# Branch B's first two weight tiles loaded at the first step of the last gate chunk, and the later ones at the first step of a chunk

## The chip, the core and the metric

The kernel runs on one core of one Trainium2 chip. The metric is the device time of one execution, in microseconds (us). "Before" is the kernel as it stands, "after" the kernel with the change.

## What is computed

One layer of a bidirectional encoder on a 1024 x 1024 float32 input (1024 tokens, model width 1024). A half-step SwiGLU feed-forward block, a normalised projection to queries, keys, values and two gates, two attention branches whose gated outputs are merged, and a second feed-forward block:

```
h = x + 0.5 * SwiGLU_1(RMSNorm(x))
u = RMSNorm(h)
[qA|kA|vA|qB|kB|vB|gA|gB] = u @ W_in
yA = NeighbourhoodAttention2D(qA, kA, vA)          # 8 heads, window in a 16 x 64 grid
yB = WindowedGQA(rope(qB), rope(kB), vB)           # 8 heads, 2 key heads, a sink logit
h = h + (sigmoid(gA) * (yA @ W_A) + sigmoid(gB) * (yB @ W_B)) @ W_out
h = h + 0.5 * SwiGLU_2(RMSNorm(h))
y = RMSNorm_final(h)
```

The part that the change touches is `sigmoid(gB) * (yB @ W_B)`: W_B is 512 x 1024 (`in_w_branch_b`), so `yB @ W_B` is a 512-deep product for 1024 outputs and 1024 tokens.

## The kernel before

**Number format.** Every large product is made of float32 operands split in two: `split` writes a rounded high part on ScalarE (ACT, line 95) and the remainder on VectorE (DVE, line 98). `mm3` (lines 146 to 153) then multiplies high by high, high by low and low by high, so that each 128 x 512 output takes three matmuls on TensorE (PE) for each 128 rows of depth: lines 149, 151 and 153.

**The attention stage.** The loop at lines 1460 to 1486 goes over 32 units of branch B and then 32 of branch A; a unit is 128 queries and one pair of heads. A turn of the loop issues the scores of unit n (`scores`: lines 1401 and 1402 on PE, the biased maximum, line 1406, on DVE, the exponential, line 1409, on ACT), the transposes of the probabilities of unit n-2 (`turn`, line 1422, with the split of the result into two tiles of the pool `ws`) and the product with the values of unit n-3 (`values`, line 1436 or 1441). Between them `filling` draws steps from a second stream, `filler` (lines 1305 to 1327), which keeps PE supplied with dense matmuls.

**The second stream.** `filler` first runs `gate(dc, steps)` for the chunks of the two gates that are still to be made. A chunk is 128 outputs of `u @ W_in`; it has eight steps, each one `mm3` over two banks (six matmuls of 512 columns). `steps` names what else is issued behind a step, mostly loads for later. The last gate chunk loads what branch B needs: the gate of its first chunk (`fetch_gate`), four pieces of yB (`fetch_y`, line 1236, split by `split_y` into `ar` tiles) and weights (`fetch_w`, line 1263). Then `branch_b` runs eight chunks `dc` of 128 outputs of `yB @ W_B`, four steps each. Chunk `dc` reads the weight tile `mix["w", dc]`, and at its end line 1294 multiplies its two banks by the opened gate. Two chunks of branch A are begun in the same way.

**Weight tiles.** Their split parts were made early in the kernel and parked in device memory (`wab_d`). `fetch_w(i)` takes one of the eight buffers of the pool `ws` and loads 128 x 1024 floats (512 KB) from `wab_d[i]`. The same eight buffers hold the two weight tiles of a gate chunk and the tiles that `turn` writes.

**Queues.** Loads and stores that are written `nc.sync.dma_start` are issued by SyncE (SP) one after the other: when one has to wait for its buffer or for the data it reads, all behind it wait too. Stores of finished gate chunks (line 1223) and the loads of branch A's heads (lines 1185 and 1188) are issued by GpSimd (POOL) in the same manner. The order on each engine's queue is set when the kernel is built, by a scheduler that takes the program's order and the buffers' release into account.

Names used below: "the first tile", "the second tile" and so on are the weight tiles of branch B's chunks dc = 0, 1, ...; in the trace all of them are `ws<-wab_d`.

Of the kernel before, what the change touches and what calls it, by code (L numbers as in the profile page):

```python
# [15 lines left out]
P = 128  # L16
# [15 lines left out]
def f32v(ap):  # L32
    return ap.bitcast(F32)
# [3 lines left out]
def trunk_kernel(ctx, tc, x, xt, n1, wg1, wu1, wd1, nm, win, rpb, sink, wa, wb, wo,  # L37
# [35 lines left out]
    def new_ar(g, dt=F32R):  # L73
        ar[g] = main.tile([P, 4, 1024], dt, tag=f"ar{g}", bufs=1, name=nm_("ar"))
        return ar[g]
# [4 lines left out]
    def bank(tag):  # L80
        return ps.tile([P, 512], F32, tag=tag, name=nm_(tag))

    def raw4():
        return main.tile([P, 1024], F32, tag="raw", bufs=4, name=nm_("raw"))

    def xs4():
        return main.tile([P, 1024], F32, tag="xs", bufs=2, name=nm_("xs"))

    def ws4():
        return main.tile([P, 1024], F32R, tag="ws", bufs=8, name=nm_("ws"))  # L90
# [55 lines left out]
    def mm3(banks, first, last, lhs, rhs, **kw):  # L146

        for b, r in zip(banks, rhs):
            nc.tensor.matmul(b, lhs[0], r[0], start=first, stop=False, **kw)  # L149
        for b, r in zip(banks, rhs):  # L150
            nc.tensor.matmul(b, lhs[0], r[1], start=False, stop=False, **kw)  # L151
        for b, r in zip(banks, rhs):
            nc.tensor.matmul(b, lhs[1], r[0], start=False, stop=last, **kw)  # L153

    def drain(gen, n=1 << 30):

        for _ in range(n):
            if next(gen, gen) is gen:
                return
# [949 lines left out]
    def gate_load(k):  # L1109
        hl = [ws4() for _ in range(2)]  # L1110
        for a, src in zip(hl, (wg_d[k, 0], wg_d[k, 1])):
            nc.sync.dma_start(f32v(a), src)
        mix["gate"] = [a.rearrange("p (c f) -> p c f", f=P) for a in hl]
# [93 lines left out]
    def u_half(c, n):  # L1207
        h, l = rhs(((B11, T4), (B21, B22))[c // 4][n])
        return h[:, c % 4, :], l[:, c % 4, :]

    def gate(dc, steps):

        w = mix.pop("gate")
        bs = [bank("g"), bank("g")]
        for k, c in enumerate((4, 5, 6, 7, 0, 1, 2, 3)):
            mm3(bs, k == 0, k == NC8 - 1, (w[0][:, c, :], w[1][:, c, :]), [u_half(c, n) for n in range(2)])
            yield
            if k in steps:
                steps[k]()
        gt = xs4()  # L1220
        for n in range(2):
            nc.scalar.copy(gt[:, n * 512:(n + 1) * 512], bs[n])
        nc.gpsimd.dma_start(g_d[dc * P:(dc + 1) * P, :], gt)
# [3 lines left out]
    def branch_mm(bs, w, y):  # L1227

        for c in range(4):
            mm3(bs, c == 0, c == 3, (w[0][:, c, :], w[1][:, c, :]),  # L1230
                [[slot(k)[:, n * 512:(n + 1) * 512] for k in y[c]] for n in range(2)])
            yield

    def fetch_y(r0):
        mix["y", r0] = raw4()
        nc.sync.dma_start(mix["y", r0], y_d[r0:r0 + P, :])

    def split_y(slots, r0, eng):

        h, l = [slot(k) for k in slots]  # L1240
        r = mix.pop(("y", r0))
        if r0 < 512:
            r = in_block(r)
            h, l = by_block(h), by_block(l)
        split(h, l, r, eng, True)
# [3 lines left out]
    def branch_a(i):  # L1249

        bs = [bank("dg"[i % 2]) for _ in range(2)]
        a_mm.append((bs, branch_mm(bs, mix.pop(("w", NC8 + i)), Y_A)))

    def merged(dc):
        return slot((0, 1, 2, 3, 24, 25, 26, 27)[dc])

    def fetch_gate(dc):
        r = mix["rb", dc] = xs4() if dc % 3 else masks[:, :1024]
        nc.sync.dma_start(r, g_d[D + dc * P:D + (dc + 1) * P, :])

    def fetch_w(i):
        t = ws4()
        nc.sync.dma_start(f32v(t), wab_d[i])
        mix["w", i] = [t[:, k:k + 512].rearrange("p (c f) -> p c f", f=P) for k in (0, 512)]

    def open_gate(dc):
        r = mix["rb", dc]
        pin(nc.scalar.activation(r, r, AF.Tanh, scale=0.5))

    def branch_b():  # L1270

        for g in (0, 6):
            new_ar(g, F32)
        fetch_w(1)
        for dc in range(NC8):
            bs = [bank("g") for _ in range(2)]
            mm = branch_mm(bs, mix.pop(("w", dc)), Y_B)
            for c in range(4):
                drain(mm, 1)
                yield  # L1280
                if c == (0 if dc else 2) and dc + 2 < NC8:
                    fetch_gate(dc + 2)
                if c == 0 and dc == 0:
                    split_y(Y_B[3], 3 * P, nc.vector)
                if c == 1:
                    if dc == 0:
                        open_gate(0)
                    fetch_w(dc + 2)
                elif c == 3 and dc + 1 < NC8:
                    open_gate(dc + 1)  # L1290
            rb = mix.pop(("rb", dc))
            for n in range(2):
                sl = slice(n * 512, (n + 1) * 512)
                nc.vector.scalar_tensor_tensor(out=merged(dc)[:, sl], in0=rb[:, sl], scalar=1.0, in1=bs[n],
                                               op0=ALU.add, op1=ALU.mult)

    def a_fetch(i):
        mix["ra", i] = raw4()
        nc.sync.dma_start(mix["ra", i], g_d[a_order[i] * P:(a_order[i] + 1) * P, :])

    def a_open(i):
        r = mix["ra", i]
        pin(nc.scalar.activation(r, r, AF.Tanh, scale=0.5))

    def filler():
        for dc, nxt in zip(gates, gates[1:] + [None]):
            if nxt is not None:
                yield from gate(dc, {2: lambda: gate_load(gates.index(nxt))})
            else:
                yield from gate(dc, {0: lambda: fetch_gate(0),  # L1310
                                     1: lambda: [fetch_y(c * P) for c in range(2)],
                                     2: lambda: [fetch_y(2 * P), fetch_w(0)],
                                     3: lambda: split_y(Y_B[0], 0, nc.vector),
                                     4: lambda: [split_y(Y_B[1], P, nc.vector), fetch_y(3 * P)],
                                     5: lambda: fetch_gate(1),
                                     6: lambda: split_y(Y_B[2], 2 * P, nc.vector)})
        yield from branch_b()
        for i in range(2):
            branch_a(i)
            for c in range(3):  # L1320
                drain(a_mm[i][1], 1)
                yield
                if c == 0:
                    fetch_w(NC8 + 2 + i)
                    a_fetch(i)
        for i in range(2):
            a_open(i)

    fill = filler()


# [345 lines left out]
```

## Time and profile before

| what | value |
|---|---|
| median of 3 runs | 1925.99 us (1922.42 to 1926.06) |
| the profiled execution | 1925.74 us |
| its span, from the first to the last instruction | 1924.0 us |
| mean granted TensorE clock | 0.997 |
| PE busy | 1910.7 us, 99% of the span |
| DVE, ACT, POOL busy | 1455.9, 947.1, 306.3 us |

The page of the profile gives busy time by engine, the chain of work that ended last, the costliest groups of instructions with the idle time ahead of them, and DMA traffic. The trace also answers which instruction waited for which, what stood on an engine in a given stretch of time, and how busy each engine was there, with the granted clock. Times in such rows are microseconds from the span's start. PE, PEld, DVE, ACT, POOL and SP are the engines; SPq is SP's queue. 1.74 us of the profiled execution lie outside its span.

### The profile page before, as it was taken

What the parts mean: (1) busy time and instruction counts of PE and PEld (TensorE: products, weight loads), DVE (VectorE), ACT (ScalarE), POOL (GpSimd) and SP (SyncE); (2) the same over time, 40 slices, a digit from 0 to 9 for tenths busy, and PEclk for the clock granted to TensorE, in tenths of its full rate; (3) what the DMA queues carried; (4) which work ended last, traced back from release to release, by engine and by line L of the source; (5) the groups of instructions that cost most, each with busy time, mean ns of one, the idle gap of its engine ahead of it and who ended that gap; (6) DMA issues with size and microseconds to landing.
All of it is one profiled execution on the core that took longest, in us unless ns stands there. A gap on an engine that the chain in (4) does not pass through costs nothing.

```text
span 1924.0 us, 25681 instructions
## 1 busy us (share of the span) xinstructions
PE 1910.7 (99%) x8908; PEld 1595.2 (83%) x8908; DVE 1455.9 (76%) x2551; ACT 947.1 (49%) x1852; POOL 306.3 (16%) x476
## 2 busy tenths in 40 slices
PE   9999999999999999999999999999999999999998
PEld 7888888888888888888898888888888888888886
DVE  8988766668967878645888897999675566569864
ACT  7533444444446543434888784475333333344453
POOL 0012222214400112211112101010110001005210
PEclk9999999999999999999999999999999999999999
DMA  6256656687454367734448968543432323492341
GB/s 268 94 174 220 232 193 224 199 294 263 125 171 142 114 203 240 237 110 151 150 117 227 254 190 313 178 156 121 148 107 102 121 88 109 148 357 93 117 141 60
DMA packets 165538, 334.36 MB, mean 174 GB/s; under 512 B 17056, under 2 KB 70688, under 8 KB 165408
## 3 DMA queue, kind: packets, MB, share of 16 engines
q1 hardware_dynamic: 132736, 233.08, 37.2%
q0 software_dynamic: 31952, 98.59, 15.4%
q8 instruction: 70, 1.15, 0.3%
q10 hardware_dynamic: 720, 1.05, 0.1%
q14 instruction: 60, 0.49, 0.1%
HBM read 228.33 MB, written 106.10 MB: 174 GB/s over the span
## 4 chain that ended last, share of the span: by engine, by line
PE 96%; DVE 2%; DMA 1%; issue 0%; ACT 0%; SPq 0%; POOLq 0%; POOL 0%; DVEq 0%
PE g L149 18%; PE g L151 17%; PE g L153 17%; PE d L149 12%; PE d L153 12%; PE d L151 12%; PE d L1422 2%; PE g L1441 1%; PE d L1401 1%; PE g L1436 1%; PE d L1402 1%; DMA ws<-wab_d 1%; PE d L142 1%; DVE ar L98 0%; DMA fx<-in_xt_dram 0%
## 5 line engine op out<-in xcount | busy, mean ns | idle before, releaser
L149 PE MATMUL g<-ar,ws 128*128 128x512 f32 x1096 | 419.4, 394 | 3.4 <-DMA ws<-wab_d 3.4
L151 PE MATMUL g<-ar,ws 128*128 128x512 f32 x1096 | 415.6, 391 | 0.1
L153 PE MATMUL g<-ar,ws 128*128 128x512 f32 x1096 | 414.2, 391 | 0.0
L149 PE MATMUL d<-ar,ws 128*128 128x512 f32 x752 | 291.3, 391 | 0.4 <-ACT ar L889 0.2
L151 PE MATMUL d<-ar,ws 128*128 128x512 f32 x752 | 290.4, 389 | 0.3 <-DVE ar L891 0.3
L153 PE MATMUL d<-ar,ws 128*128 128x512 f32 x752 | 290.3, 389 | 0.2 <-DVE ws L322 0.2
L151 PEld LDWEIGHTS g<-ar,ws 128*128 128x128 f32 x1096 | 206.0, 188 | 41.9 <-DVE ar L98 0.3
L153 PEld LDWEIGHTS g<-ar,ws 128*128 128x128 f32 x1096 | 205.7, 188 | 42.2
L149 PEld LDWEIGHTS g<-ar,ws 128*128 128x128 f32 x1096 | 203.1, 188 | 40.8 <-issue 3.7
L322 DVE TENSOR_TENSOR ws<-raw,ws 128x512 fp32r<-128x512 f32 x222 | 151.8, 689 | 94.7 <-ACT ws L319 93.8
L319 ACT CAST ws<-raw 128x512 fp32r<-128x512 f32 x222 | 136.3, 620 | 152.1 <-PE g L153 70.0
L149 PEld LDWEIGHTS d<-ar,ws 128*128 128x128 f32 x752 | 141.0, 188 | 30.5 <-ACT ar L889 0.6
L151 PEld LDWEIGHTS d<-ar,ws 128*128 128x128 f32 x752 | 141.2, 188 | 30.1 <-DVE ar L891 0.9
L153 PEld LDWEIGHTS d<-ar,ws 128*128 128x128 f32 x752 | 141.2, 188 | 29.8 <-DVE ws L322 0.7
L95 ACT CAST ws<-raw 128x512 fp32r<-128x512 f32 x98 | 61.0, 622 | 119.8 <-PE d L153 61.4
L98 DVE TENSOR_TENSOR ws<-raw,ws 128x512 fp32r<-128x512 f32 x98 | 74.0, 755 | 43.5 <-ACT ws L95 43.4
L426 POOL DMA_DIRECT2D hid<-fx x91 | 49.1, 540 | 349.9 <-DVE fx L486 237.7
L98 DVE TENSOR_TENSOR ws<-ar,ws 128x512 fp32r<-128x512 f32 x114 | 93.6, 828 | 14.5 <-ACT ws L95 14.5
L95 ACT CAST ar<-raw 128x512 fp32r<-128x512 f32 (+1 forms) x81 | 54.1, 670 | 84.3 <-PE g L151 51.4
L149 PE MATMUL g<-ws,ws 128*128 128x512 f32 x232 | 90.9, 392 | 0.0
L153 PE MATMUL g<-ws,ws 128*128 128x512 f32 x232 | 90.4, 390 | 0.0
L151 PE MATMUL g<-ws,ws 128*128 128x512 f32 x232 | 90.3, 389 | 0.0
(325 smaller groups left out, 3678.5 us busy)
## 6 DMA issues: line engine op xcount, KB each, us to landing
raw<-hid SPq DMA_DIRECT2D x70, 512.0 KB
hid<-fx POOLq DMA_DIRECT2D x91, 256.0 KB, 2.9
ar<-in_ffn_w_down_dram SPq DMA_DIRECT2D x32, 512.0 KB
raw<-in_ffn_w_up_dram SPq DMA_DIRECT2D x31, 512.0 KB
raw<-in_ffn_w_gate_dram SPq DMA_DIRECT2D x27, 512.0 KB
hid<-fa POOLq DMA_DIRECT2D x51, 256.0 KB, 2.7
ar<-zs_d POOLq DMA_DIRECT2D x48, 256.0 KB, 6.7
raw<-in_w_in_dram SPq DMA_DIRECT2D x20, 512.0 KB
```

Of the source, the lines that this page charges most:

```text
L95: hi = nc.scalar.copy(dst_hi, src)
L98: (eng or nc.vector).tensor_tensor(dst_lo, src, f32v(dst_hi), op=ALU.subtract)
L142: nc.tensor.transpose(pt[:, c * P:(c + 1) * P], xs[:, (half * 4 + c) * P:(half * 4 + c + 1) * P], ident)
L149: nc.tensor.matmul(b, lhs[0], r[0], start=first, stop=False, **kw)
L151: nc.tensor.matmul(b, lhs[0], r[1], start=False, stop=False, **kw)
L153: nc.tensor.matmul(b, lhs[1], r[0], start=False, stop=last, **kw)
L319: nc.scalar.copy(w[0][:, :512], a)
L322: nc.vector.tensor_tensor(w[0][:, 512:], a, f32v(w[0][:, :512]), op=ALU.subtract)
L426: nc.gpsimd.dma_start(hid[PRODUCTS.index(p), i], src)
L1401: nc.tensor.matmul(b[:, :nw], un["q"][s], un["kd"][s][:, k0 * P:k1 * P], start=True, stop=False)
L1402: nc.tensor.matmul(b[:, :nw], un["q"][s], un["kl"][s][:, k0 * P:k1 * P], start=False, stop=True)
L1422: nc.tensor.transpose(pt[:, i * P:(i + 1) * P], un["pr"][s][:, i * P:(i + 1) * P], ident)
```

## The change

In the last gate chunk the loads of branch B's first and second weight tile are both issued behind the first step (step 0), with the load of the gate. Before, the first tile was loaded behind the third step and the second at the start of `branch_b`, after the eighth step. In `branch_b` the load of tile dc + 2 moves from the second step of chunk dc to the first.

```diff
@@ branch_b
         for g in (0, 6):
             new_ar(g, F32)
-        fetch_w(1)
         for dc in range(NC8):
...
                 if c == 0 and dc == 0:
                     split_y(Y_B[3], 3 * P, nc.vector)
-                if c == 1:
-                    if dc == 0:
-                        open_gate(0)
+                if c == 1 and dc == 0:
+                    open_gate(0)
+                if c == 0:
                     fetch_w(dc + 2)
                 elif c == 3 and dc + 1 < NC8:
                     open_gate(dc + 1)
@@ filler
             else:
-                yield from gate(dc, {0: lambda: fetch_gate(0),
+                yield from gate(dc, {0: lambda: [fetch_gate(0), fetch_w(0), fetch_w(1)],
                                      1: lambda: [fetch_y(c * P) for c in range(2)],
-                                     2: lambda: [fetch_y(2 * P), fetch_w(0)],
+                                     2: lambda: fetch_y(2 * P),
                                      3: lambda: split_y(Y_B[0], 0, nc.vector),
```

The only queue whose order changes is SP's; PE, DVE, ACT and POOL issue the same instructions in the same order as before. Lines behind 1274 have a number lower by one after the change (1372 is 1371, and so on). This is SP's queue in the last gate chunk and up to the third tile, before; `ws_9175` is the first tile, `ws_9380` the second, `ws_9472` the third, and `xs_9522` the gate of the third chunk:

```order
L1236 DMA raw_9123<-y_d 128x1024
L1236 DMA raw_9125<-y_d 128x1024
L1236 DMA raw_9173<-y_d 128x1024
L1259 DMA xs_9302<-g_d 128x1024
L1263 DMA ws_9175<-wab_d 128x1024
...
L1191 DMA raw_9964<-z_d 128x1024
L1263 DMA ws_9380<-wab_d 128x1024
L1259 DMA xs_9522<-g_d 128x1024
L1263 DMA ws_9472<-wab_d 128x1024
L1372 DMA y_d<-fa 64x2x512
```

The same places on SP's queue after the change, where `ws_9091` is the first tile, `ws_9093` the second and `ws_9438` the third:

```order
L1236 DMA raw_9127<-y_d 128x1024
L1236 DMA raw_9129<-y_d 128x1024
L1263 DMA ws_9091<-wab_d 128x1024
L1263 DMA ws_9093<-wab_d 128x1024
L1236 DMA raw_9177<-y_d 128x1024
L1259 DMA xs_9304<-g_d 128x1024
...
L1191 DMA raw_9966<-z_d 128x1024
L1259 DMA xs_9522<-g_d 128x1024
L1263 DMA ws_9438<-wab_d 128x1024
L1371 DMA y_d<-fa 64x2x512
```

The first tile goes ahead of two loads, the second ahead of ten; the third tile stays where it was, behind the gate's load `xs_9522`. Further down the queue, from chunk 4 on, the load of a weight tile and that of a gate change places, at chunk 6 also a weight tile and a store; the rows from there, before:

```order
L1236 DMA raw_10312<-y_d 128x1024
L1259 DMA masks_5583<-g_d 128x1024
L1263 DMA ws_10139<-wab_d 128x1024
L1372 DMA y_d<-fa 64x2x512
L1259 DMA xs_10244<-g_d 128x1024
L1263 DMA ws_10292<-wab_d 128x1024
```

The same rows after the change:

```order
L1236 DMA raw_10312<-y_d 128x1024
L1263 DMA ws_10072<-wab_d 128x1024
L1259 DMA masks_5583<-g_d 128x1024
L1371 DMA y_d<-fa 64x2x512
L1263 DMA ws_10246<-wab_d 128x1024
L1259 DMA xs_10244<-g_d 128x1024
```

Here the weight tile moves one place ahead of a gate's load. On PE the order is unchanged; these are the first matmuls of branch B's second chunk, behind the scores of an attention unit, before:

```order
L1402 MATMUL d_9512<-ar_5099,ar_564 128x384
L149 MATMUL g_9547<-ar_4722,ws_9380 128x512
L151 MATMUL g_9547<-ar_4722,ws_9380 128x512
L153 MATMUL g_9547<-ar_4722,ws_9380 128x512
L1422 MATMUL d_9532<-ident,fa 128x128 x3
```

The same rows after the change:

```order
L1401 MATMUL d_9512<-ar_5099,ar_564 128x384
L149 MATMUL g_9547<-ar_4722,ws_9093 128x512
L151 MATMUL g_9547<-ar_4722,ws_9093 128x512
L153 MATMUL g_9547<-ar_4722,ws_9093 128x512
L1421 MATMUL d_9532<-ident,fa 128x128 x3
```

They read the second tile, which is `ws_9380` before and `ws_9093` after; nothing else differs.

## The prediction

> **What bounds the kernel now.** I read the page first, for the engine that sets the end:
>
> ```profile
> span 1924.0 us, 25681 instructions
> PE 1910.7 (99%) x8908; PEld 1595.2 (83%) x8908; DVE 1455.9 (76%) x2551; ACT 947.1 (49%) x1852; POOL 306.3 (16%) x476
> PE 96%; DVE 2%; DMA 1%; issue 0%; ACT 0%; SPq 0%; POOLq 0%; POOL 0%; DVEq 0%
> L149 PE MATMUL g<-ar,ws 128*128 128x512 f32 x1096 | 419.4, 394 | 3.4 <-DMA ws<-wab_d 3.4
> ```
>
> PE is busy for 99% of the span and is 96% of the chain that ended last. A change elsewhere counts only where it takes away a time in which PE stands still. The last row names one: of all the idle time ahead of line 149's gate matmuls, 3.4 us were ended by the landing of a weight tile `ws<-wab_d`, which is what the change moves. Next I asked PE's waits, to see whether that is one wait or many:
>
> ```profile
> PE g L149 <- DMA ws<-wab_d: 3.4, 1, 3.4
> PE g L810 <- POOL ident masks.py:199: 1.5, 1, 1.5
> PE d L151 <- DVE ar L891: 0.3, 1, 0.3
> ```
>
> The columns are total, count and longest. It is one wait of 3.4 us, the longest in the kernel. PE's timeline shows where it is, with start, duration and, in brackets, the idle time and what ended it:
>
> ```profile
> 1071.19 0.33 PE L1401 MATMUL d<-ar,ar 128*128 128x384 f32 x1
> 1071.36 0.34 PE L1402 MATMUL d<-ar,ar 128*128 128x384 f32 x1
> 1075.13 0.77 PE L149 MATMUL g<-ar,ws 128*128 128x512 f32 x1 [3.43 <-DMA ws<-wab_d]
> 1075.69 0.63 PE L151 MATMUL g<-ar,ws 128*128 128x512 f32 x1
> 1076.12 0.63 PE L153 MATMUL g<-ar,ws 128*128 128x512 f32 x1
> ...
> 1081.01 0.39 PE L151 MATMUL g<-ar,ws 128*128 128x512 f32 x1
> 1081.24 0.39 PE L153 MATMUL g<-ar,ws 128*128 128x512 f32 x1
> ...
> 1089.93 0.40 PE L149 MATMUL g<-ar,ws 128*128 128x512 f32 x1
> ```
>
> The matmul at 1075.13 is the first of branch B's second chunk; the one at 1089.93 is the first of the third chunk, which starts without a wait. Two things are lost at 1071. PE stands still, and then it runs slowly: from L151 to L153 takes 0.43 us at 1075.69 and 0.23 us at 1081.01. The stage table has the granted clock beside it (columns: stretch, length, busy time of PE, PEld, DVE, ACT and POOL, clock, DMA share, GB/s):
>
> ```profile
> 1066.00:1071.50 5.50, 5.44 (x31) 4.46 (x29) 5.11 (x13) 5.43 (x14) 0.00 (x0) 1.00 1.09 361
> 1071.36:1075.13 3.77, 0.34 (x3) 0.05 (x2) 2.92 (x10) 1.84 (x4) 0.00 (x0) 0.87 1.38 239
> 1075.13:1081.01 5.88, 5.88 (x17) 4.84 (x18) 2.52 (x6) 3.59 (x8) 0.00 (x0) 0.50 0.95 262
> 1081.01:1089.93 8.92, 8.92 (x61) 8.09 (x59) 6.02 (x19) 6.31 (x18) 0.14 (x1) 1.00 0.63 210
> 1071.36:1089.93 18.57, 15.14 (x79) 12.98 (x78) 11.45 (x34) 11.73 (x29) 0.14 (x1) 0.82 0.88 232
> ```
>
> The clock is 0.50 for 5.88 us behind the wait and 1.00 before and after. Last, the chain in order of time, and then SP's timeline, say which load it was:
>
> ```profile
> 1058.45 16.55 DMA ws<-wab_d
> 1074.99 0.14 issue
> ```
>
> ```profile
> 1040.20 1.28 SPq L1236 DMA_DIRECT2D raw<-y_d  x3
> 1041.65 0.91 SPq L1259 DMA_DIRECT2D xs<-g_d  x1
> 1042.68 0.53 SPq L1263 DMA_DIRECT2D ws<-wab_d  x1
> ...
> 1058.45 0.37 SPq L1263 DMA_DIRECT2D ws<-wab_d  x1
> 1070.55 0.32 SPq L1259 DMA_DIRECT2D xs<-g_d  x1
> 1070.97 0.37 SPq L1263 DMA_DIRECT2D ws<-wab_d  x1
> 1071.44 0.70 SPq L1372 DMA_DIRECT2D y_d<-fa  x1
> 1082.10 0.32 SPq L1236 DMA_DIRECT2D raw<-y_d  x1
> ```
>
> The awaited load was issued at 1058.45 and took 16.55 us. On SP it is the second `ws<-wab_d` of branch B: the second tile, the one that the change puts at the head of the queue. The third tile went out at 1070.97.
>
> **The second tile, early.** After the change SP issues the first and second tile behind two loads of `y_d`, so at about 1041 and 1041.5, 17 us earlier than the second goes out now. PE needs it at 1071.4, some 30 us later, and even another 16.55 us would be over by 1058.1. The wait then goes. What it gives back: with the clock up, the next matmul would start 0.17 us behind L1402 at 1071.36 (the step from L1401 to L1402), so at 1071.53 and not at 1075.13: 3.60 us. The 5.88 us at half clock hold work that takes 5.88 x 0.23 / 0.43 = 3.15 us at full clock: 2.73 us. Together 6.33 us.
>
> Of the half-clock stretch the Trainium skill (TensorE: Matmul & The Clock Gate, section on Part 1, the HAM clock gate) says that the clock comes back after some 3.4 us of sustained matmuls. By that the second part would be an estimated 1.7 us and the gain 5.3. The trace shows 5.88 us at 0.50, so the sum keeps 2.73.
>
> **What takes the wait's place on PE.** ACT and DVE must keep up through the same instructions. Over 1071.36 to 1089.93 PE would need 18.57 - 6.33 = 12.24 us; ACT is busy for 11.73 and DVE for 11.45. That is 96% and 94%, tight, but before the wait ACT was busy for 5.43 of 5.50 us (99%) and PE did not wait. ACT's and DVE's long idle times in this stretch come from PE's own:
>
> ```profile
> 1077.42 0.48 ACT L95 CAST ws<-d 128x384 fp32r<-128x384 f32 x1 [3.94 <-PE d L1422]
> 1077.94 0.56 DVE L98 TENSOR_TENSOR ws<-d,ws 128x384 fp32r<-128x384 f32 x1 [3.66 <-ACT ws L95]
> ```
>
> ACT waited 3.94 us for PE's transposes, and DVE 3.66 us for ACT. With PE running on, both vanish. The cost lies between 0 and what they would keep of their idle time; I take 0.3 us, near the lower end, by the row at 99% without a wait. That leaves 6.33 - 0.3 = 6.0 us.
>
> **What is moved back.** On SP two issues go ahead of the third `y_d` load, the gate's load and the bias loads: about 0.43 us each (three issues in 1.28), nothing of it on PE. Their data, 1.05 MB, go ahead too. A full stretch moves
>
> ```profile
> DMA packets 596, 2.09 MB, mean 418 GB/s; under 512 B 64, under 2 KB 103, under 8 KB 595
> ```
>
> in 5 us (1045 to 1050), so the third `y_d` piece lands 2.5 us later and the rest 1.25 us later (the first tile was among them anyhow). The pieces of `y_d` are read from
>
> ```profile
> 1065.38 1.04 ACT L95 CAST ar<-raw 128x1024 fp32r<-128x1024 f32 x1
> ```
>
> 24 us behind the issue at 1041, so 0. Were that cover gone, the price would be at most those 2.5 us. SP could also stand at the first tile until a buffer of `ws` is free:
>
> ```profile
> SPq L1263 <- PE g L1436: 13.5, 6, 5.1
> SPq L1259 <- DMA g_d<-xs: 11.7, 1, 11.7
> SPq L1236 <- DMA y_d<-fa: 18.1, 3, 9.8
> ```
>
> The longest wait of that kind now is 5.1 us (first row); behind it stand the same loads, with the same cover, so between 0 and 5.1 us on SP and 0 on PE.
>
> **The third tile and later ones.** Its program place is earlier, but on SP it still stands behind the gate's load of 1070.55, which waited 11.7 us for POOL's store of the last gate chunk (second row). So it goes out at about 1071 as now. Behind it in the queue is the store of 1071.44, and the load of 1082.10 waited for that store's landing (third row; 9.8 us from the issue before it). So the third tile was in by about 1082.1, even with the second one's 512 KB ahead of it, which are now gone from there. PE needs it at 1089.93 - 6.33 = 1083.6: cover of at least 1.5 us. All other weight tiles go out at the same place or earlier, and PE waits for none of them now: 0.
>
> Sum: 1925.74 - 6.0 = **1919.7 us**, made against the profiled execution, which is 0.25 us under the median of the runs (1925.99). The measurement of this kernel can tell about 0.2% (3.9 us) from no change.
>
> **Rivals.** *ACT and DVE hold PE back.* For it speaks the 96%; against it the rows without waits at 99%. If ACT keeps half of its idle time in this stretch (18.57 - 11.73 = 6.84, half is 3.4), the stretch takes 11.73 + 3.4 = 15.1 us instead of 12.24, and the gain is 3.4: 1922.3.
>
> *The third tile takes the second one's place, and it is slower.* SP reaches it only when POOL's store has landed, and it needs no more than the second tile's 16.55 us to miss: 1070.97 + 16.55 = 1087.5, a wait of 3.9 us and again 2.7 at half clock, 6.6 against 6.33 saved: 1926.0, no change. If the tiles that now load early hold up POOL's store by 3 us more, it lands at 1090.5, the wait is 6.9 and the sum 9.6: 1929.0. It decides against the change from a landing later than 1083.6 + 3.6 = 1087.2. Against it: the bound of 1082.1, and 512 KB less in the queue.
>
> **Chances.** The forecast 0.77, the first rival 0.10, the third tile as late as 1087 0.05, later than that 0.08. The forecast and a little of the first rival make faster by over 0.2%: 0.78. The rest of the first rival (1922.3 is 0.19% under the median) and the tile at 1087 make no difference: 0.14. Slower: 0.08. For the range, the low end is the whole 6.33 and half of the spread of the three runs (3.64 / 2 = 1.8): 1917.6, rounded to 1917.5. The high end takes in the first rival, 1922.3, with 0.7 for that spread: 1923.0. Outside are the second rival, 0.13, and some 0.06 at the ends.
>
> **What would show it.** Right: no row `PE g L149 <- DMA ws<-wab_d` among PE's waits, a clock of 1.00 from 1060 to 1090, the first matmul of the third chunk near 1083.6 to 1084, a span near 1918. In SP's timeline the two first tiles go out within 2 us of 1041. Wrong in size: PE waits of some tenths on DVE or ACT behind 1071, with the third chunk's start later than 1085. Wrong altogether: a row of 3 us or more for `ws<-wab_d` at the third chunk, with the clock at 0.50 behind it, or a wait on `ar` near 1066.

## The result and the profile after

The changed kernel takes 1920.01 us (median of 13 runs) against 1924.99 us for the kernel before (13 runs beside it). The ratio is 0.9974, with a 95% interval of 0.9966 to 0.9983: 5.0 us less, between 3.3 and 6.5. One execution of 2259.9 us, at a granted clock of 0.794, is left out of the ratio; the others of the changed kernel lie between 1918.82 and 1922.11, those of the kernel before between 1922.42 and 1928.51. The profiled execution took 1920.27 us.

The page and PE's waits of the changed kernel, the rows that answer to those of before:

```profile
span 1918.5 us, 25682 instructions
PE 1909.1 (100%) x8908; PEld 1593.7 (83%) x8908; DVE 1455.8 (76%) x2551; ACT 947.1 (49%) x1852; POOL 305.6 (16%) x476
L149 PE MATMUL g<-ar,ws 128*128 128x512 f32 x1096 | 418.3, 393 | 0.0
PE g L810 <- POOL ident masks.py:199: 1.5, 1, 1.5
PE d L151 <- DVE ar L891: 0.3, 1, 0.3
```

The span is 5.5 us shorter. PE's busy time is 1.6 us less for the same 8908 matmuls, and the stretch at half clock behind the wait is gone. The idle time ahead of line 149 is 0.0 where it was 3.4, and the row for `ws<-wab_d` among PE's waits is gone; the longest wait that is left, 1.5 us at the kernel's start, was there before.

PE's timeline at the start of the second chunk, and at that of the third (start, duration):

```profile
1072.25 0.34 PE L1401 MATMUL d<-ar,ar 128*128 128x384 f32 x1
1072.42 0.40 PE L149 MATMUL g<-ar,ws 128*128 128x512 f32 x1
...
1084.44 0.40 PE L149 MATMUL g<-ar,ws 128*128 128x512 f32 x1
```

The first product of the second chunk starts 0.17 us behind the score matmul. From there to the third chunk it takes 1084.44 - 1072.42 = 12.02 us; before it was 1089.93 - 1075.13 = 14.80. The stage table over the same place (length, busy time of PE, PEld, DVE, ACT and POOL, clock, DMA share, GB/s):

```profile
1066.00:1071.36 5.36, 5.28 (x31) 4.53 (x31) 4.98 (x13) 5.31 (x12) 0.27 (x1) 1.00 1.24 341
1071.36:1083.60 12.24, 12.24 (x77) 10.89 (x76) 11.87 (x37) 11.46 (x29) 0.00 (x0) 1.00 0.93 205
```

PE is busy for all of the 12.24 us and the clock is 1.00. DVE is at 97% and ACT at 94%, and PE waits for neither. SP's timeline shows where the loads went:

```profile
1041.06 0.81 SPq L1236 DMA_DIRECT2D raw<-y_d  x2
1041.96 1.46 SPq L1263 DMA_DIRECT2D ws<-wab_d  x2
1043.47 0.55 SPq L1236 DMA_DIRECT2D raw<-y_d  x1
...
1072.10 0.32 SPq L1259 DMA_DIRECT2D xs<-g_d  x1
1072.52 0.37 SPq L1263 DMA_DIRECT2D ws<-wab_d  x1
```

The first two tiles go out at 1041.96 and 1042.45 (the row above merges them), the third one at 1072.52.

### The profile page after: what moved, and what is told of

It is laid out like the page before. It is cut to its first block, busy times and chain, and to the rows that moved or that the text cites. A ratio compares the mean times of both kernels' runs of the same rounds, so it can differ in the third digit from the quotient of the medians.

```text
span 1918.5 us, 25682 instructions
## 1 busy us (share of the span) xinstructions
PE 1909.1 (100%) x8908; PEld 1593.7 (83%) x8908; DVE 1455.8 (76%) x2551; ACT 947.1 (49%) x1852; POOL 305.6 (16%) x476
## 3 DMA queue, kind: packets, MB, share of 16 engines
q8 instruction: 70, 1.15, 0.2%
## 4 chain that ended last, share of the span: by engine, by line
PE 97%; DVE 2%; DMA 0%; issue 0%; ACT 0%; SPq 0%; POOLq 0%; POOL 0%; DVEq 0%
PE g L151 18%; PE g L149 18%; PE g L153 18%; PE d L149 12%; PE d L153 12%; PE d L151 12%; PE d L1421 2%; PE d L1400 1%; PE g L1440 1%; PE g L1435 1%; PE d L1401 1%; PE d L142 1%; DVE ar L98 0%; DMA fx<-in_xt_dram 0%; PE d L1199 0%
```

## Experiments: is it the second tile alone?

**The kernel before, once more.** No edit.

> The kernel before, once more, for a second look at the stall. If the stall belongs to the program, PE again waits for the second weight tile of branch B, between 2.5 and 4 us, and runs behind it at a clock of 0.50 for 5 to 7 us. If the 3.4 us of the first profile were a chance of that execution, the wait is under 2 us here and the clock stays at 1.00.

Measured: 1928.57 us, one execution. PE's wait in it, and the load that ended it from the chain (issue, duration):

```profile
1078.11 0.76 PE L149 MATMUL g<-ar,ws 128*128 128x512 f32 x1 [5.56 <-DMA ws<-wab_d]
1059.28 18.69 DMA ws<-wab_d
```

The stall belongs to the program, but its size does not. The load took 18.69 us here against 16.55 in the first profile, and the wait was 5.56 us against 3.43.

**The second tile early, nothing else.**

```
-        fetch_w(1)
...
-                yield from gate(dc, {0: lambda: fetch_gate(0),
+                yield from gate(dc, {0: lambda: [fetch_gate(0), fetch_w(1)],
```

> Half of the change alone: the second weight tile of branch B at the first step of the last gate chunk; the first one stays at its third step, and the later ones at the second step of a chunk, as before. My theory (all of the gain is the second tile's landing): no wait for ws<-wab_d on PE at 1071, the clock 1.00 there, and 5 to 6.4 us less than before, the same as the whole change. The rival (the first tile's place or the later tiles bring part of it): a gain of 3 us or less, or a wait for the first or the third tile.

Measured: 1919.96 us against 1925.71 for before on the same chip, ratio 0.9967 (0.9955 to 0.9980). In its profile PE waits for no tile, and the only wait over 0.3 us is the 1.5 us at the kernel's start that all of them have. This part of the change is worth all of it.

**The later tiles early, nothing else.**

```
-                if c == 1:
-                    if dc == 0:
-                        open_gate(0)
+                if c == 1 and dc == 0:
+                    open_gate(0)
+                if c == 0:
                     fetch_w(dc + 2)
```

> The other half alone: branch B's later weight tiles at the first step of a chunk; the first and second tile as before. My theory: 0. PE waits 3.4 us for the second tile as before and then runs at 0.50 for some 6 us; the time is that of before within 1 us. The rival (the later tiles carry a part of the gain): 2 us or more below before.

Measured: 1926.42 us against 1925.71, ratio 1.0003 (0.9994 to 1.0011). PE's wait is still there:

```profile
1076.21 0.47 PE L149 MATMUL g<-ar,ws 128*128 128x512 f32 x1 [3.85 <-DMA ws<-wab_d]
```

The later tiles' part is worth nothing that can be measured. The third part, the first tile's new place, was not run alone; with that tile in its old place the second tile's load gave the whole gain, so nothing is left for it to explain.

## Experiments: how early is early enough?

**Four places earlier on SP, and one.** In the kernel before, the second tile's load leaves the head of branch B and goes to the sixth step of the last gate chunk (ahead of a bias load, a store and two loads of `z_d`), or to the seventh (ahead of the last load of `z_d` alone):

```
-        fetch_w(1)
...
-                                     5: lambda: fetch_gate(1),
+                                     5: lambda: [fetch_gate(1), fetch_w(1)],
```

```
-        fetch_w(1)
...
-                                     6: lambda: split_y(Y_B[2], 2 * P, nc.vector)})
+                                     6: lambda: [split_y(Y_B[2], 2 * P, nc.vector), fetch_w(1)]})
```

> The kernel before with the second tile only one to four loads earlier on SP: at the sixth step of the last gate chunk, ahead of a bias load, the store of y_d and two loads of z_d that it stood behind. In the profile of before those landed from 1061 to 1071; the tile would take their place and land near 1066 to 1069. My theory (a tile that lands before 1071 is as good as one that lands at 1050): no wait of PE for it, clock 1.00, 1920 us like the whole change. The rival (it must be out of this queue altogether): a wait of 1 us or more remains, 1921.5 or above.

> The kernel before with the second tile exactly one load earlier on SP: the seventh step of the last gate chunk, it changes places with the load of z_d of 1058.01, which landed 3.9 us ahead of it in the first profile (1071.1 and 1075.0). It should land 1 to 2.5 us sooner and leave a wait of 1 to 2.5 us. My theory (the clock drops only where PE stood still for most of one period of 3.4 us): clock 1.00 throughout, only the wait remains, 1921 to 1922.5. The rival of my prediction (half clock of 2.7 us behind any wait): 1923.7 to 1925.2. If PE doesn't wait at all the time is that of the whole change, 1920, and this says nothing on the clock.

Measured: 1920.96 us, ratio 0.9970 (0.9960 to 0.9981), for the sixth step and 1920.90 us, ratio 0.9975 (0.9965 to 0.9986), for the seventh, against 1925.99. Neither profile has a wait for a tile. PE's waits, SP's timeline and one of SP's waits of the second one:

```profile
PE g L810 <- POOL ident masks.py:199: 1.5, 1, 1.5
PE d L151 <- DVE ar L891: 0.5, 2, 0.3
...
1055.83 0.55 SPq L1263 DMA_DIRECT2D ws<-wab_d  x1
1057.95 0.32 SPq L1191 DMA_DIRECT2D raw<-z_d  x1
1069.96 0.32 SPq L1259 DMA_DIRECT2D xs<-g_d  x1
...
SPq L1191 <- DVE s L1365: 1.8, 1, 1.8
```

A change of places with one load of the same size is enough. I had expected a wait of 1 to 2.5 us to be left, by the 3.9 us between the two landings; the load also went out at 1055.83 instead of 1058.45, since SP's wait at that load of `z_d` (1.8 us here, the last row) now stands behind the tile and not ahead of it. How much each of the two brings was not separated. Being this near may have a price: one of the eight runs took 1923.6 us, where nine of the whole change end at 1922.2 (the last experiment). That run has no trace, so a late tile in it is not shown. The test of the clock that this run was also meant for gave nothing, since PE did not wait.

## Experiments: what a late tile costs

**Work in the place of the wait.** 14 products more ahead of the second chunk's first one, and then 7, in the kernel before. Products and other work around them also change places on PE, DVE and ACT, so only the clock, the wait and the sum are read here.

```
             mm = branch_mm(bs, mix.pop(("w", dc)), Y_B)
+            for _ in range(14 if dc == 1 else 0):
+                nc.tensor.matmul(bs[0], slot(4)[:, :P], slot(4)[:, :512], start=True, stop=True)
```

> The kernel before with 14 products more, 128x128 by 128x512, ahead of the second chunk's first one; they write a bank that the chunk's own first product overwrites. They are some 3.2 us of PE's work where PE would wait 3.4 us, and they don't bring the tile earlier. My theory (the stall costs twice: 3.6 us of standing still and 2.7 us of half clock): the tile lands at 1075 as before, but the clock stays at 1.00 behind it, and the time is 2 to 3 us below before in spite of the work added. The rival (the half clock is no consequence of the stand-still, or PE's clock comes down with any late load): clock 0.50 behind the landing as before, and a time equal to before or up to 3.2 us above. If the added products are spread so that PE still stands for over 2.5 us, the test says nothing.

Measured: 1922.46 us against 1925.71, ratio 0.9983 (0.9974 to 0.9992): more work, and a shorter time. The stage table, with the wait:

```profile
1077.43 0.73 PE L149 MATMUL g<-ar,ws 128*128 128x512 f32 x2 [0.61 <-DMA ws<-wab_d]
...
1073.80:1077.21 3.41, 3.02 (x16) 2.20 (x14) 3.11 (x11) 3.39 (x8) 0.00 (x0) 1.00 1.37 240
1077.21:1080.62 3.41, 3.19 (x19) 2.89 (x20) 1.75 (x4) 1.43 (x3) 0.00 (x0) 1.00 1.05 261
```

The tile is as late as ever (PE starts on it at 1077.43), but the clock stays at 1.00. So the half clock is a consequence of PE's standing still, and it is a cost of its own. (The profiled execution, 1924.31 us, is the slowest of the eleven.)

> The kernel before with 7 products more ahead of the second chunk's first one, half of the 14 of the other run; the chunk's own first product overwrites what they write. They are some 1.6 us of PE's work, so of the waits of 3.4 to 5.6 us seen so far 1.8 to 4 us should be left. My theory (the clock drops at the end of one of its periods of 3.41 us in which PE worked for about a third or less, and for nothing shorter): with a wait up to 1.6 us the clock stays at 1.00; with one of 1.8 to 2.2 us it drops only if nearly all of it lies in one period; with more it drops as before, for one or two whole periods, 3.4 or 6.8 us. The time between that of 14 products (1922.5) and before (1925.7). The rival (any wait over 0.6 us is followed by half clock for about as long again): 0.50 behind each of them, its length going with the wait.

Measured: 1923.69 us against 1926.40, ratio 0.9989 (0.9980 to 0.9998), between the two as expected. In the profiled execution (1925.79 us) a wait of 2.84 us was left:

```profile
1077.38 0.51 PE L149 MATMUL g<-ar,ws 128*128 128x512 f32 x1 [2.84 <-DMA ws<-wab_d]
...
1074.80:1078.21 3.41, 0.83 (x4) 0.69 (x5) 2.76 (x8) 2.80 (x7) 0.00 (x0) 1.00 1.25 233
1078.21:1081.62 3.41, 3.41 (x13) 3.03 (x12) 1.13 (x4) 0.02 (x1) 0.00 (x0) 0.50 0.88 307
1081.62:1085.03 3.41, 3.41 (x24) 3.14 (x23) 1.66 (x5) 2.64 (x8) 0.00 (x0) 1.00 0.36 116
```

The stretches are cut where the clock changes. It came down at 1078.21, 0.8 us after PE had gone back to work, and it went up again 3.41 us later. That is not a clock that falls when PE stops and rises when it starts.

**The second tile later still.** Its load behind the gate's load at 1070.6:

```
-        fetch_w(1)
...
                     split_y(Y_B[3], 3 * P, nc.vector)
+                    fetch_w(1)
```

> The kernel before with the second tile made later still: its load stands behind the gate's load at 1070.6 on SP, directly ahead of the third tile's. It would land near 1081, a wait of PE of 8.5 to 10 us instead of 3.4. My theory (the half clock has a size of its own: it ends at the end of the first period of 3.4 us in which PE was busy throughout, 3.4 to 6.8 us behind the restart, and so costs 1.6 to 3.2 us however long the wait was): a clock of 0.50 from about 2.5 us into the wait until 3.4 to 6.8 us behind its end, and a time 5 to 7 us above before, about 1931. The rival (the half clock grows with the wait, 2.7 us for each 3.6): 10 us or more above, 1936.

Measured: 1929.42 us against 1924.99, ratio 1.0023 (1.0014 to 1.0032). The wait, the load, and the stretches:

```profile
1078.91 0.76 PE L149 MATMUL g<-ar,ws 128*128 128x512 f32 x1 [6.27 <-DMA ws<-wab_d]
1071.60 7.17 DMA ws<-wab_d
...
1072.74:1076.16 3.42, 0.00 (x0) 0.00 (x0) 2.48 (x10) 1.56 (x2) 0.00 (x0) 1.00 1.18 238
1076.16:1079.57 3.41, 0.66 (x2) 0.59 (x3) 0.00 (x0) 0.00 (x0) 0.00 (x0) 0.50 1.01 402
1079.57:1082.99 3.42, 3.42 (x13) 2.74 (x12) 0.76 (x2) 1.78 (x5) 0.00 (x0) 0.50 0.44 140
1082.99:1086.40 3.41, 3.41 (x22) 2.99 (x21) 2.98 (x9) 2.78 (x6) 0.00 (x0) 1.00 0.10 38
```

The time is 4.4 us above before, under the 5 to 7 of the theory and far from the 10 of the rival. I had the wait too long: 6.27 us, not 8.5 to 10, since the load took 7.17 us from its issue at 1071.60 where the one issued at 1058.45 took 16.55. The clock came back as the theory said, 4.1 us behind the restart, at the end of the first period in which PE was busy throughout. The wait is 2.8 us longer than in the first profile, and PE's work at half clock is shorter: 0.66 + 3.42 = 4.08 us.

**The clock goes by periods of 3.41 us.** The same cuts in the first profile of before, in its second one, and in that of the later tiles alone:

```profile
1070.74:1074.15 3.41, 0.96 (x5) 0.55 (x3) 3.35 (x12) 2.46 (x5) 0.00 (x0) 1.00 1.40 257
1074.15:1077.57 3.42, 2.44 (x7) 1.94 (x8) 0.13 (x2) 0.15 (x1) 0.00 (x0) 0.50 1.19 219
1077.57:1080.98 3.41, 3.41 (x11) 2.93 (x10) 2.49 (x6) 3.41 (x8) 0.00 (x0) 0.50 0.81 294
```

```profile
1069.92:1073.33 3.41, 2.63 (x14) 1.99 (x12) 3.35 (x9) 3.05 (x10) 0.00 (x0) 1.00 1.20 299
1073.33:1076.75 3.42, 0.00 (x0) 0.00 (x0) 1.80 (x7) 1.01 (x2) 0.00 (x0) 1.00 1.42 234
1076.75:1080.14 3.39, 2.03 (x7) 1.67 (x7) 0.00 (x0) 0.00 (x0) 0.00 (x0) 0.50 1.10 255
1080.14:1083.54 3.40, 3.40 (x12) 2.83 (x11) 2.07 (x5) 3.14 (x8) 0.00 (x0) 0.50 0.58 212
```

```profile
1070.54:1073.95 3.41, 1.83 (x9) 1.25 (x7) 3.35 (x11) 3.07 (x7) 0.00 (x0) 1.00 1.32 269
1073.95:1077.36 3.41, 1.15 (x7) 0.99 (x8) 0.98 (x5) 0.19 (x1) 0.00 (x0) 1.00 1.29 233
1077.36:1080.76 3.40, 3.40 (x13) 2.84 (x12) 2.19 (x6) 3.25 (x8) 0.00 (x0) 0.50 0.99 325
```

Read each row as a period: what PE did in it decides the clock of the next. Behind periods in which PE was busy for 0, 0.83, 0.96 and 1.15 of 3.41 us the clock is 0.50; behind those with 1.83 and 2.63 us it stayed at 1.00. Once at 0.50, it stays there behind periods with 0.66, 2.03 and 2.44 us of work and goes back behind those that were busy throughout.

The trace also keeps the times at which the granted clock changed, and they show that the periods form one grid through the whole execution. In the first profile of before the clock rose at 5.78 us, fell at 1074.15, rose at 1080.98 and fell behind PE's last work at 1920.66: 313, 315 and 561 periods of 3.4133 us after the first rise. In all thirteen traces every later change lies within 0.01 us of a whole number of periods behind the first. The end of the kernel, where PE runs out of work, narrows the limit. These are the last periods there of the run with the tile one place earlier, and of the run with the third tile late (below):

```profile
1909.92:1913.33 3.41, 1.38 (x7) 0.80 (x5) 1.44 (x2) 1.45 (x3) 0.76 (x3) 1.00 0.41 154
1913.33:1916.74 3.41, 0.00 (x0) 0.00 (x0) 0.75 (x1) 0.72 (x1) 0.35 (x1) 0.50 0.41 154
```

```profile
1909.19:1912.60 3.41, 1.66 (x8) 1.04 (x6) 1.44 (x2) 1.45 (x3) 0.76 (x3) 1.00 0.41 154
1912.60:1916.01 3.41, 0.00 (x0) 0.00 (x0) 0.75 (x1) 0.72 (x1) 0.55 (x1) 1.00 0.41 156
```

Behind 1.38 us of work the clock fell, behind 1.66 us it stayed. The way back does not need a full period either: at the start of the execution with the second tile later still, a period with 2.84 us of work came ahead of the first rise at 4.37 us (14 matmuls of line 810 in these 2.84 us; behind the rise 16 took 1.80).

Where the grid lies differs from execution to execution: the first rise comes 4.4 to 7.1 us from the span's start. So where the wait falls in a period is chance, and PE worked 3.4 to 5.9 us at half clock, and not more behind a longer wait: 5.85 us behind 3.43, 4.08 behind 6.27.

With the prediction's factor (0.43 us at half clock for 0.23) each us worked at half clock costs 1 - 0.23 / 0.43 = 0.465 us. The wait is taken as the idle time in the row and 0.17 us, since the next matmul would have started 0.17 us ahead of the recorded end of the one before it. From the 1920.15 us that the changed kernel took (last experiment), and with this wait, 0.23 us for each added product and 0.465 of the time worked at half clock, the profiled executions come out so (us):

```
                        added  wait   at half   sum   reckoned  measured
before, first profile   0      3.60   5.85      6.3   1926.5    1925.74
before, second profile  0      5.73   5.43      8.3   1928.4    1928.57
later tiles alone       0      4.02   3.40      5.6   1925.8    1925.84
7 products              1.61   3.01   3.41      6.2   1926.4    1925.79
14 products             3.22   0.78   0         4.0   1924.2    1924.31
second tile later       0      6.44   4.08      8.3   1928.5    1929.29
```

All six lie within 0.8 us, as near as can be asked where the changed kernel itself spreads by 2.9 us. The sum is checked on these executions only, and it does not fit the median of the 14 products: 1922.46 is 2.3 us above the changed kernel, less than the 3.2 us of the products alone. The work that changed places beside them may make up the rest; that is not shown.

## Experiments: the third tile's cover

**The third tile early too, and late.** In the changed kernel, its load at the first step of the last gate chunk as well, or at the first step of the second chunk:

```
-                if c == 0:
+                if c == 0 and dc:
                     fetch_w(dc + 2)
...
-                yield from gate(dc, {0: lambda: [fetch_gate(0), fetch_w(0), fetch_w(1)],
+                yield from gate(dc, {0: lambda: [fetch_gate(0), fetch_w(0), fetch_w(1), fetch_w(2)],
```

```
                 if c == 0:
-                    fetch_w(dc + 2)
+                    for i in ((), (2, 3), (4,))[dc] if dc < 3 else (dc + 2,):
+                        fetch_w(i)
```

> The changed kernel with the third tile too at the first step of the last gate chunk. My theory (the third tile has cover of some 3 us where it is now, so nothing is left to win): the time of the changed kernel within 1 us, no wait of PE for any tile. The rivals: the third tile is late in some runs, then up to 2 us faster; or one tile more ahead of the y_d pieces and one more buffer held make PE wait on ar near 1066 or hold up SP, 1 to 5 us slower.

Measured: 1920.27 us, ratio to before 0.9974 (0.9964 to 0.9984), the time of the changed kernel beside it (1920.15). No wait for a tile; nothing was left to win, and the third buffer held cost nothing that can be measured.

> The changed kernel with the third tile made late on purpose: its load stands behind SP's load of y_d at 1082, at the first step of the second chunk. It would go out near 1082.6 and land 3.3 to 4.2 us later, at 1086 to 1087, where PE needs it at 1084.4. My theory (a late tile costs its wait, and half clock on top only where PE has stood still for most of one of the clock's periods of 3.4 us): PE waits 1.5 to 2.5 us, the clock mostly stays at 1.00, and the time is 1.5 to 2.5 us above the changed kernel, about 1922. The rival of my prediction (any such wait brings 2.7 us of half clock with it): 4.2 to 5.2 us above it, about 1924.5.

Measured: 1920.52 us, ratio 0.9975 (0.9966 to 0.9984). No wait, and the clock stayed up: neither my theory nor the rival was tested, since the tile was not late. SP's timeline says why:

```profile
1070.54 0.32 SPq L1259 DMA_DIRECT2D xs<-g_d  x1
1071.89 0.60 SPq L1372 DMA_DIRECT2D y_d<-fa  x1
1078.30 0.32 SPq L1236 DMA_DIRECT2D raw<-y_d  x1
1078.71 0.38 SPq L1263 DMA_DIRECT2D ws<-wab_d  x1
```

The load of `y_d` that I had put it behind waits for the store of 1071.89 to land. It went out at 1078.30 and not at 1082.2, and the tile with it. One reason could be that the tile's 512 KB no longer stand directly ahead of that store, but this is not shown: with the third tile loaded early they don't stand there either, and the load still went out only at 1080.88.

**The changed kernel once more**, on the same chip as these.

> The changed kernel once more, beside the next three on the same chip. My theory: 1920 us, and a spread of about 2 us between its runs where the kernel before has 6, since the tile whose landing moves from run to run is out of the way. The rival: the spread is the chip's and not the tile's, 4 us or more here as well.

Measured: 1920.15 us (nine runs from 1919.23 to 1922.16) against 1924.99 (28 runs from 1922.67 to 1928.87), ratio 0.9974 (0.9965 to 0.9984). The spread is 2.9 us against 6.2, so about half of it was the tile. I had expected about 2. This profile is the slowest of the nine, 1.9 us above that of the changed kernel shown first (1920.27), and small waits of PE make up 1.7 of it. The largest are

```profile
PE d L151 <- DVE ar L891: 0.6, 2, 0.3
PE d L151 <- DVE ws L98: 0.4, 1, 0.4
PE d L1199 <- DVE nmx L1406: 0.4, 1, 0.4
```

## Why the prediction was right

The forecast was 1919.7 us, and 1920.0 was measured. That the two are this near is in part luck: the forecast took 6.0 us off a profiled execution of 1925.74, and the medians differ by 5.0 us from a kernel before of 1924.99. The 1.0 us too much and a start 0.75 us too high nearly cancel.

- **The second tile.** Right, and it is all of the gain: alone it gives a ratio of 0.9967, the whole change 0.9974, and the later tiles alone 1.0003. The wait is gone.
- **The size of 6.33 us.** Right for the execution that it was read from: in the profiled pair the span is 5.5 us shorter, and the execution after came to this place 0.9 us later than the one before (its last score matmul at 1072.25, before at 1071.36), so 6.4 us came back here. But it is no constant of the kernel. The wait was 3.4, 3.9 and 5.6 us in three executions with the load in its old place, and the half clock cost 1.6, 2.5 or 2.7. The medians differ by 4.8 to 5.8 us over the comparisons of the changed kernel and of the second tile's part alone. I had put the spread of the kernel before into the range as noise of the measurement; by the last experiment about half of it was the very wait that I was pricing.
- **The half clock, 2.73 us.** Right for its execution, for a reason that I did not have. I set the trace's 5.88 us against the 3.4 us of the Trainium skill (TensorE: Matmul & The Clock Gate, section on Part 1, the HAM clock gate) as if one had to be wrong. The same section says that the window of about 3.4 us is free-running and is not reset when a kernel starts. The runs agree: the first profile had a period of 2.44 us of work and a full one (3.41) at half clock, two other runs one full period (3.40 and 3.41), and the grid of 3.4133 us began at another place in each execution. Worked out from the shorter case, 3.60 + 1.58 = 5.2 us would have stood beside 6.33 as the other end. The table in that section of the Trainium skill has the clock go down after an idle window; here PE worked for up to 1.38 of the 3.41 us and it still went down.
- **ACT and DVE, 0.3 us.** It was 0: DVE was busy for 97% and ACT for 94% of the 12.24 us, and PE waited for neither. The rival that had them hold PE back is out.
- **What is moved back.** Right in the 0 for PE: it waits for no `y_d` piece. The two issues held the third piece back by 1.5 us on SP (1041.96 to 1043.47), not by 0.86, and the cover took it up.
- **The third tile.** Right: it went out at 1072.52, 1.55 us later than before, of which 0.9 us is that this execution ran late, and PE did not wait at 1084.44. Loading it earlier gains nothing, and sending it out at 1078.7, in a queue that let it through sooner, costs nothing. How large its cover is stays open: the bound of 1.5 us took it that what stands ahead of a store in the queue has landed when the store has, and no row shows this tile's landing. The rival of a late third tile is out; how it would have ended with a really late one was not seen.
- **What would show it.** Four signs are there: no wait row, clock 1.00, a span of 1918.5 us, and both tiles out within 2 us of 1041. The fifth was missed by 0.4 us: the third chunk started at 1084.44 and not by 1084, in an execution that had come to this place 0.9 us late.

No version that was run beats the changed kernel by what can be measured; it has 1.8 us of named waits on PE left, in the two rows shown.

## What to carry to other kernels

A single wait on the bounding engine that ends with a load is worth taking away by issue order alone, and it takes little: here one place in the queue did as well as ten (nine loads and a store) by the medians, perhaps with less room. Price it from more than one execution, since a load's landing in a full queue moves by microseconds, and add the half clock by the periods of the clock rather than in proportion to the wait. When a load is moved, ask which store or load behind it goes earlier for that: twice here a load that was sent later was less late than reckoned, once because the load itself was faster (7.17 us for 16.55) and once because the load ahead of it went out 4 us sooner.

## What the runs showed of the hardware

- The clock changes only at the ends of periods of 3.4133 us that run on whatever PE does, from the first rise to the kernel's end (thirteen traces); in one execution it fell 0.8 us after PE had gone back to work. A period with 1.38 us of PE's work did not keep it up, one with 1.66 us did; 2.44 us did not bring it back, 2.84 us did.
- The same load of 512 KB took 16.55, 17.00 and 18.69 us from issue to landing in three executions with the same queue, and 7.17 us when it was issued some 13 us later, behind the gate's load.
